# Keeping the low parts of weights in DRAM between the two halves of a two-layer decoder step

## The chip, the cores and the metric

The program runs on one core of one Trainium2 chip. The metric is the device time of one execution in microseconds (us), from start to end, with all weights read from DRAM. TensorE (PE) does the matrix products, VectorE (DVE), ScalarE (ACT) and GpSimd (POOL) the element work, and SyncE (SP) issues nearly all DMA transfers, one after the other in a fixed order.

## The reference, cut to what matters

Two layers are applied to 1024 prompt positions and 64 sample positions (1088 columns, T below). Layer 0 is an S5 state-space mixer and a gated delta network side by side; layer 1 is RWKV-7 time mixing. Each mixer is followed by a SwiGLU feed-forward network (FFN) of width 2816. Everything is in float32.

```python
def swiglu(h, w_gate, w_up, w_down):
    return (jax.nn.silu(h @ w_gate) * (h @ w_up)) @ w_down

for layer in range(2):
    h = rmsnorm(x, norm_mix[layer])
    mix = s5_and_gdn(h) if layer == 0 else rwkv7(h)   # each with input and output projections
    x = x + mix
    h = rmsnorm(x, norm_ffn[layer])
    x = x + swiglu(h, w_gate[layer], w_up[layer], w_down[layer])
y = rmsnorm(x, norm_final)
```

## The kernel before, in words

**Split products.** To reach float32 accuracy with TensorE's fp32r type, each operand is split: a high part that is the value rounded to fp32r, and a low part that is what the rounding left. A product is then three: high x high, high weight x low activation, low weight x high activation (`mm`, L301). So each weight tile that is loaded is split on chip. `weight` (L280) does this: SP loads the raw tile (L285) into one of two buffers `raw`, ACT rounds it into `wh` (L289), and POOL, or DVE where `lo=v` is given, subtracts to get `wl` (L290). `wh` and `wl` have three buffers for most weights; those of the down projection, named `wdh` and `wdl`, have two (L529).

**Two halves.** The 1088 columns are worked in two halves, `HALF` (L23): columns 0 to 511 as two chunks of 256, and 512 to 1087 as two chunks of 288. After the input stage of layer 0 (to about 456 us), the first loop of `trunk` (`for s in range(2)`) takes one half at a time through the output side of layer 0 (GLU, `wout`, FFN 0) and then the RWKV projections `wk`, `wr`, `wv` and the small low-rank weights `w1`, `a1`, `g1`. The second loop takes one half at a time through `wo` and FFN 1. Every weight is thus loaded and split twice, once for each half. By the weight loads of the trace the first half of loop one runs from 456 to 1359 us, the second from 1359 to 2435 us; loop two's halves run from 2435 to 3210 and from 3210 us to the end.

**FFN.** `ffn` (L455 on) works on 22 blocks of 128 hidden units. For each block there is a gate and an up weight, 128x1024 each (512 KB, matmuls `pg`); after each three blocks comes a down step with eight weights of 128x384 (192 KB, matmuls `pd`), in all seven such groups of eight and a last step with two large tiles. In FFN 0's first half DVE makes the `wdl` of these groups (`alone` is true, L529), in its second half POOL does.

**RWKV units.** While FFN 0's second half runs, the units of the RWKV scan of the first half are worked beside it (`unit`), and while FFN 1's first half runs, those of the second half. A unit loads its inputs (`rkb`, `th`, `ta`, `k`, `r`, `v`, about L1540 to L1549), inverts small triangular blocks with a chain of short DVE operations (L172 and L174, with round trips through DRAM: `dA`, `L`, `dT`, `Tc`), and then takes turns between PE and the other engines (L1652 to L1669).

**What sets the order.** The program is not written in the order in which it runs: a list scheduler simulates the engines and fixes the order of each engine's instructions when the program is built. On the chip each engine then takes its instructions strictly in that order, each waiting for the semaphores it names. A DMA on SP that waits therefore holds all that stand behind it.

Of the kernel before, what the change touches and what calls it, by code (L numbers as in the profile page):

```python
# [8 lines left out]
F32 = mybir.dt.float32  # L9
# [22 lines left out]
class Fine:  # L32


    def __init__(self, nc, pool, shape, ring=12, slots=None):
        self.nc, self.v, self.pool, self.shape, self.ring, self.n = nc, nc.vector, pool, list(shape), ring, 0
        self.slots = slots
# [38 lines left out]
    def log1p(self, out, e):  # L76

        v = self.v
        m, t, x = self.tmp(), self.tmp(), self.tmp()
        v.tensor_scalar(m, e, 0.41421356, None, op0=OP.is_gt)  # L80
        v.tensor_scalar(t, e, 0.5, 0.5, op0=OP.mult, op1=OP.add)
        v.tensor_mul(t, t, m)
        v.tensor_sub(x, e, t)
        p = self.horner(x, [7.0376836292e-2, -1.1514610310e-1, 1.1676998740e-1, -1.2420140846e-1, 1.4249322787e-1,
                            -1.6668057665e-1, 2.0000714765e-1, -2.4999993993e-1, 3.3333331174e-1, -0.5])
        v.tensor_mul(p, p, x)
        v.scalar_tensor_tensor(p, m, 0.69314718056, p, op0=OP.mult, op1=OP.add)
        v.tensor_add(out, p, x)


class Kern:
# [187 lines left out]

    def weight(self, src, kt=8, m=128, tag="w", bufs=3, lo=None):  # L280

        nc = self.nc
        raw = self.dp.tile([128, 1024], F32, tag="raw", name="raw", bufs=2)
        raw = raw[:, :kt * m].rearrange("p (k m) -> p k m", m=m)
        nc.sync.dma_start(raw, src)  # L285
        p = self.dx if tag == "wd" else self.dp
        wh = p.tile([128, kt, m], F32R, tag=tag + "h", name=tag + "h", bufs=bufs)
        wl = p.tile([128, kt, m], F32R, tag=tag + "l", name=tag + "l", bufs=bufs)
        nc.scalar.copy(wh, raw)  # L289
        (lo or nc.gpsimd).tensor_sub(wl, raw, wh)  # L290
        return wh, wl

    def mm(self, ps, w, x, cn, c=0):
# [1606 lines left out]
def loaded(K, s, dy, own=None):  # L1900

    t0, W, chunks = HALF[s]
    hs = [([], []) for c in chunks]
    for i, y in enumerate(dy):
        t = K.ring("act", "yr")[:, :W]
        e = own is not None and i == len(dy) - 1
        n = W - own.shape[-1] if e else W
        K.nc.sync.dma_start(t[:, :n], y[:, t0:t0 + n])
        for (c, cn), (h, l) in zip(chunks, hs):
            (a,), (b,) = K.hilo(1)  # L1910
            m = min(max(n - c, 0), cn)
            if m:
                K.split(a[:, :m], b[:, :m], t[:, c:c + m], K.nc.gpsimd if i % 2 else None)
            if m < cn:
                K.split(a[:, m:cn], b[:, m:cn], own[:, c + m - n:c + cn - n])
            h.append(a)
            l.append(b)
    return hs
# [5 lines left out]
@with_exitstack  # L1924
def trunk(ctx, tc, *aps):
    nc = tc.nc
    I = dict(zip(IN_NAMES, aps))
    I.update({"o_" + n: a for (n, _), a in zip(OUTS, aps[len(IN_NAMES):])})
    K = Kern(ctx, tc)
    K.nv = K.const.tile([128, 4, 8], F32, name="nv")  # L1930
    dr = ctx.enter_context(tc.tile_pool(name="tkd", bufs=1, space=DRAM))
    dx = dr.tile([128, 8, T], F32, name="dx")
    dyr = [dr.tile([128, T], F32, name="dyr%d" % i) for i in range(8)]
    right = ctx.enter_context(ExitStack())
    dyg, dy, second, early = layer0(K, I, right, dr)
    K.open(ctx, 288, 4, reuse_waits="tile")

    def tail(s, src, ys, w, i, x=None, done=None, ahead=lambda: None):
        if early is not None and s == i == 0:
            early.close()  # L1940
            K.open_more(ctx, reuse_waits="tile")
        x = K.load_x(src, s, x)
        first = s == i == 0
        ready = {}

        def gate():
            ready[0, 0] = K.weight(I["wg"][i][0])

        norms = K.project(x, ys, HALF[s][2], w, (lambda: None) if first else gate, 7 if first else 8)
        if first:  # L1950
            second(ORDER[0])
            with tc.high_priority(3000):
                norms = K.project_last(x, ys, HALF[s][2], w, gate)
            second(ORDER[1])
        return x, K.ffn(x, s, norms, K.nv[:, 1 + i], I["wg"][i], I["wup"][i], I["wd"][i], ready, ahead, s == i, done)

    rw = None
    for s in range(2):
        t0, W, chunks = HALF[s]
        wk0 = []  # L1960
        keys = lambda: wk0.append(K.weight(I["wk"][0]))
        keep = lambda m, c, cn, t: nc.sync.dma_start(dx[:, m, t0 + c:t0 + c + cn], t)
        x, norms = tail(s, I["x"], mixed0(K, s, dyg, dy, I["wglu"]), I["wout"], 0, done=keep, ahead=keys)
        if rw is None:
            right.close()
            rw = RWKV(K, ctx, I["rvec"])
            rw.open(ctx)
        unit = lambda ft, si=2 * s: rw.start(ft, si, I["rs0"], I["o_rwkv"], dyr)
        rw.projections(s, x, I["rsh"], *(I[n] for n in ("w1", "a1", "g1", "lw2", "wk", "wr", "wv")), unit, norms, wk0[0])
        for ft in range(8):  # L1970
            own = unit(ft, 2 * s + 1)
    nc.sync.dma_start(I["o_shift"], rw.shift)
    for s in range(2):
        t0, W, chunks = HALF[s]
        if s:
            K.psn = rw.norm_bank
        x, (bc, r1) = tail(s, dx, loaded(K, s, dyr, own if s else None), I["wo"], 1, rw.spare() if s else None)
        with tc.issue_after(K.last.ins) if s else ExitStack():
            for i, (c, cn) in enumerate(chunks):
                K.rms([t[:, c:c + cn] for t in x], K.nv[:, 3], K.spread(r1) if i else bc,  # L1980
                      lambda k, t: nc.sync.dma_start(I["o_y"][:, k, t0 + c:t0 + c + cn], t), True,
                      ((1, 3, 5, 7), (5, 7))[i] if s else ())
# [95 lines left out]
```

## Time and profile before

| | |
|---|---|
| median of 3 runs | 3781.07 us (3778.25 to 3793.54) |
| the profiled execution | 3776.02 us, of which the instructions span 3774.2 us |
| PE busy | 3475.1 us (92%) |
| DVE, ACT, POOL busy | 2512.1, 1390.7, 1317.6 us |
| mean granted PE clock | 0.941 of full speed |
| DMA | 356.35 MB, 94 GB/s on average |

The profile is one execution. Busy time of an engine counts its own instructions; matmuls are pipelined, so the duration of one (about 300 ns) is longer than the distance to the next (about 120 to 130 ns). A granted clock of 1.00 means 2.4 GHz and 0.50 means 1.2 GHz; a stretch's figure is the mean over it. In a timeline the bracket behind a row says how long the engine had been idle and what ended that.

### The profile page before, as it was taken

What the parts mean: (1) busy time and instruction counts of PE and PEld (TensorE: products, weight loads), DVE (VectorE), ACT (ScalarE), POOL (GpSimd) and SP (SyncE); (2) the same over time, 40 slices, a digit from 0 to 9 for tenths busy, and PEclk for the clock granted to TensorE, in tenths of its full rate; (3) what the DMA queues carried; (4) which work ended last, traced back from release to release, by engine and by line L of the source; (5) the groups of instructions that cost most, each with busy time, mean ns of one, the idle gap of its engine ahead of it and who ended that gap; (6) DMA issues with size and microseconds to landing.
All of it is one profiled execution on the core that took longest, in us unless ns stands there. A gap on an engine that the chain in (4) does not pass through costs nothing. (4 is left out here: it accounts for less than half of the span.)

```text
span 3774.2 us, 77080 instructions
## 1 busy us (share of the span) xinstructions
PE 3475.1 (92%) x29894; PEld 3221.5 (85%) x29894; DVE 2512.1 (67%) x6836; ACT 1390.7 (37%) x3264; POOL 1317.6 (35%) x1189
## 2 busy tenths in 40 slices
PE   7889989999988889999999988898998999899998
PEld 6879888899978788888888877888888888799997
DVE  7876877654456477777777674577787877553444
ACT  3333433322225443434433354443443443232222
POOL 3322233222236543433333264543333333332221
PEclk9989997999988999999999988998998999899999
DMA  4424442322223552222222224721222322322222
GB/s 104 94 81 132 97 124 75 95 81 90 88 92 96 167 174 68 60 79 79 78 81 69 92 72 129 222 84 50 86 86 78 94 82 87 130 62 82 90 77 70
DMA packets 331405, 356.35 MB, mean 94 GB/s; under 512 B 133272, under 2 KB 273304, under 8 KB 331040
## 3 DMA queue, kind: packets, MB, share of 16 engines
q1 hardware_dynamic: 321824, 342.52, 30.7%
q10 hardware_dynamic: 9216, 8.92, 0.7%
q8 instruction: 235, 3.85, 0.4%
q14 instruction: 130, 1.06, 0.1%
HBM read 285.34 MB, written 64.81 MB: 93 GB/s over the span
## 5 line engine op out<-in xcount | busy, mean ns | idle before, releaser
L290 POOL TENSOR_TENSOR wl<-raw,wh 128x1024 fp32r<-128x1024 f32 (+2 forms) x301 | 701.7, 2333 | 1094.9 <-ACT wh L289 1018.1
L301 PE MATMUL pg<-hi,wh 128*128 128x288 f32 (+1 forms) x2816 | 841.0, 299 | 31.5 <-DVE s L490 17.8
L301 PE MATMUL pg<-lo,wh 128*128 128x288 f32 (+1 forms) x2816 | 836.9, 297 | 4.8 <-DVE lo L388 3.5
L301 PE MATMUL pg<-hi,wl 128*128 128x288 f32 (+1 forms) x2816 | 835.6, 297 | 0.0
L301 PEld LDWEIGHTS pg<-hi,wh 128*128 128x128 f32 x2816 | 544.4, 193 | 43.9 <-DVE s L490 20.5
L301 PEld LDWEIGHTS pg<-lo,wh 128*128 128x128 f32 x2816 | 544.4, 193 | 14.2 <-DVE lo L388 4.7
L301 PEld LDWEIGHTS pg<-hi,wl 128*128 128x128 f32 x2816 | 544.1, 193 | 4.9 <-issue 2.1
L289 ACT CAST wh<-raw 128x1024 fp32r<-128x1024 f32 (+3 forms) x309 | 312.6, 1013 | 355.9 <-PE pg L301 88.4
L301 PE MATMUL pd<-ah,wdh 128*128 128x256 f32 (+1 forms) x1280 | 388.2, 303 | 18.6 <-DVE x L513 17.2
L301 PE MATMUL pd<-ah,wdl 128*128 128x256 f32 (+1 forms) x1280 | 373.2, 292 | 1.4 <-POOL wdl L290 1.4
L301 PE MATMUL pd<-al,wdh 128*128 128x256 f32 (+1 forms) x1280 | 371.9, 291 | 0.0
L301 PEld LDWEIGHTS pd<-ah,wdh 128*128 128x128 f32 x1280 | 243.9, 191 | 30.0 <-DVE x L513 19.6
L301 PE MATMUL pj<-lo,wh 128*128 128x256 f32 (+1 forms) x768 | 240.3, 314 | 18.8 <-DVE lo L388 15.9
L301 PE MATMUL pj<-hi,wh 128*128 128x256 f32 (+1 forms) x768 | 239.5, 314 | 14.0 <-ACT hi L387 6.0
L301 PEld LDWEIGHTS pd<-ah,wdl 128*128 128x128 f32 x1280 | 243.8, 190 | 3.4 <-POOL wdl L290 1.7
L301 PEld LDWEIGHTS pd<-al,wdh 128*128 128x128 f32 x1280 | 244.2, 191 | 1.1 <-issue 0.8
L301 PE MATMUL pj<-hi,wl 128*128 128x256 f32 (+1 forms) x768 | 234.9, 308 | 1.5 <-POOL wl L290 1.4
L513 DVE TENSOR_TENSOR x<-x,pd 128x256 f32<-128x256 f32 (+1 forms) x384 | 163.4, 427 | 87.7 <-PE pd L301 82.5
L289 ACT CAST wdh<-raw 128x384 fp32r<-128x384 f32 (+1 forms) x224 | 111.3, 497 | 247.0 <-PE pd L301 170.6
L172 DVE TENSOR_TENSOR Tm<-L,T 32x15 f32<-32x15 f32 (+8 forms) x600 | 181.7, 303 | 28.6 <-DMA L<-dA 15.3
L174 DVE TENSOR_TENSOR T<-T,Tm 32x15 f32<-32x15 f32 (+8 forms) x600 | 190.6, 318 | 13.5
L301 PE MATMUL pi<-hi,wh 128*128 128x272 f32 x640 | 192.2, 300 | 4.0 <-ACT us L1788 2.5
(643 smaller groups left out, 8275.5 us busy)
## 6 DMA issues: line engine op xcount, KB each, us to landing
raw<-in_wg SPq DMA_DIRECT2D x88, 512.0 KB
raw<-in_wup SPq DMA_DIRECT2D x88, 512.0 KB
raw<-in_wd SPq DMA_DIRECT2D x192, 192.0 KB
raw<-in_win SPq DMA_DIRECT2D x20, 512.0 KB
raw<-pr ACTq DMA_DIRECT2D x64, 136.0 KB
raw<-in_wk SPq DMA_DIRECT2D x16, 512.0 KB
raw<-in_wr SPq DMA_DIRECT2D x16, 512.0 KB
raw<-in_wv SPq DMA_DIRECT2D x16, 512.0 KB
```

What stands on the lines that cost most here:

```text
L172: v.tensor_mul(mm, L[:nl, j:j + 1, j + 1:16].to_broadcast([nl, j + 1, n]), T[:nl, 0:j + 1, j:j + 1].to_broadcast([nl, j + 1, n]))
L174: v.tensor_tensor(T[:nl, 0:j + 1, j + 1:16], T[:nl, 0:j + 1, j + 1:16], mm, op=op)
L289: nc.scalar.copy(wh, raw)
L290: (lo or nc.gpsimd).tensor_sub(wl, raw, wh)
L301: self.nc.tensor.matmul(ps, a[k], b[:, c:c + cn], start=i == 0, stop=i == last)
L513: v.tensor_add(x[m][:, c:c + cn], x[m][:, c:c + cn], ps)
```

## The change

A class `Kept` pairs a weight in DRAM with a second DRAM tensor of the same shape for its low part. The first time round, `weight` does what it did and then stores `wl` there with one more DMA on SP. Once the flag `there` is set, which the end of the first half of loop one does (for `wo`, its second use), `weight` loads `wl` from DRAM by SP in place of the subtraction; the raw tile is still loaded and ACT still rounds it. This concerns `wglu`, `wout`, `w1`, `a1`, `g1`, `wk`, `wr`, `wv`, `wo` and the three weights of FFN 0. FFN 1's weights are handled as before. In the built program 309 DMAs are added on SP, and 152 subtractions on POOL and 2 on DVE are gone.

```diff
+class Kept:
+    def __init__(self, src, low, root=None):
+        self.src, self.low, self.root = src, low, root or self
+        self.there = False
+    def __getitem__(self, i):
+        return Kept(self.src[i], self.low[i], self.root)
...
     def weight(self, src, kt=8, m=128, tag="w", bufs=3, lo=None):
         nc = self.nc
+        kept, src = (src, src.src) if isinstance(src, Kept) else (None, src)
         raw = self.dp.tile([128, 1024], F32, tag="raw", name="raw", bufs=2)
...
         nc.scalar.copy(wh, raw)
+        if kept and kept.root.there:
+            nc.sync.dma_start(wl.bitcast(F32), kept.low)
+            return wh, wl
         (lo or nc.gpsimd).tensor_sub(wl, raw, wh)
+        if kept:
+            nc.sync.dma_start(kept.low, wl.bitcast(F32))
         return wh, wl
...
+    both = ["wglu", "wout", "w1", "a1", "g1", "wk", "wr", "wv", "wo"]
+    for n in both:
+        I[n] = Kept(I[n], dr.tile(list(I[n].shape), F32, name="low_" + n))
+    for n in ("wg", "wup", "wd"):
+        I[n] = [Kept(I[n][0], dr.tile(list(I[n].shape[1:]), F32, name="low_" + n)), I[n][1]]
...
         for ft in range(8):
             own = unit(ft, 2 * s + 1)
+        for w in [I[n] for n in both[:-1]] + [I[n][0] for n in ("wg", "wup", "wd")]:
+            w.there = True
...
     for s in range(2):
         t0, W, chunks = HALF[s]
+        I["wo"].there = s > 0
```

The scheduler orders all engines anew. Three places follow. In the changed kernel the line numbers are higher: the raw load is L301, the load of a low part L307, the subtraction L309 and the store L311; the RWKV unit's lines are 21 higher.

The first is SP in a down group of FFN 0's first half, before and then changed; `wdl` is a low part of the down weight, `low_wd` its place in DRAM.

```order
L285 DMA raw<-in_wd 128x384 [waits DMAHW0_49,DVE_49]
L285 DMA raw<-in_wd 128x384 [waits DMAHW1_49,DVE_49]
L285 DMA raw<-in_wup 128x1024 [waits DMAHW2_49,DVE_49]
L285 DMA raw<-in_wg 128x1024 [waits DMAHW3_49,DVE_49]
L285 DMA raw<-in_wup 128x1024 [waits DMAHW4_49,Pool_49]
```

```order
L311 DMA low_wd<-wdl 128x384 [waits DMAHW2_49,DVE_49]
L301 DMA raw<-in_wd 128x384 [waits DMAHW7_49,Activation_49]
L311 DMA low_wd<-wdl 128x384 [waits DMAHW4_49,DVE_49]
L301 DMA raw<-in_wup 128x1024 [waits DMAHW1_49,Activation_49]
L311 DMA low_wd<-wdl 128x384 [waits DMAHW6_49,DVE_49]
L301 DMA raw<-in_wg 128x1024 [waits DMAHW3_49,Activation_49]
L311 DMA low_wup<-wl 128x1024 [waits DMAHW0_49,Pool_49]
```

A store now stands ahead of each raw load. It waits for the subtraction for which the raw load waited before.

The second is SP in a down group of FFN 0's second half, with the loads of an RWKV unit (`rkb` to `v`) among the weights, before and then changed.

```order
L285 DMA raw<-in_wd 128x384 [waits DMAHW5_49,Pool_49]
L178 DMA Tc<-dT 128x4x16 [waits DMAHW7_49,DMAHW1_49]
L1544 DMA rkb<-dks_13312 64x256 [waits DMAHW2_49,DVE_49,Pool_49]
L1544 DMA rkb<-dks_13312 64x256 [waits DMAHW3_49]
L1548 DMA th<-dth 128x256 [waits DVE_49]
L1549 DMA ta<-dta 128x256 [waits Activation_49]
L1540 DMA k<-dk 128x256 [waits DMAHW6_49,PE_49]
L1540 DMA r<-drr 128x256 [waits DVE_49]
L1540 DMA v<-dv 128x256 [waits DMAHW0_49,DVE_49]
L285 DMA raw<-in_wd 128x384 [waits DMAHW1_49,Pool_49]
```

```order
L307 DMA wdl<-low_wd 128x384 [waits DMAHW4_49,DMAHW0_49,PE_49]
L301 DMA raw<-in_wd 128x384 [waits DMAHW5_49,DMAHW1_49,Activation_49]
L1565 DMA rkb<-dks_13440 64x256 [waits DVE_49,Pool_49]
L1565 DMA rkb<-dks_13440 64x256
L1569 DMA th<-dth 128x256 [waits Activation_49]
L1570 DMA ta<-dta 128x256 [waits DVE_49]
L1561 DMA k<-dk 128x256 [waits DMAHW6_49,PE_49]
L1561 DMA r<-drr 128x256 [waits DMAHW7_49,DVE_49]
L1561 DMA v<-dv 128x256 [waits DMAHW0_49,DVE_49]
L307 DMA wdl<-low_wd 128x384 [waits DMAHW1_49]
L301 DMA raw<-in_wup 128x1024 [waits DMAHW2_49,Activation_49]
L307 DMA wdl<-low_wd 128x384 [waits DMAHW3_49,PE_49]
```

Before, only raw loads stand around the unit's loads; now a low part that PE has still to multiply by stands behind them, and each low part waits for PE to free its buffer.

The third is POOL beside the same units, before and then changed.

```order
L290 TENSOR_TENSOR wdl<-raw,wdh 128x384
L1588 TENSOR_TENSOR BK<-kp,Pi 64x4x64 x2
L290 TENSOR_TENSOR wdl<-raw,wdh 128x384
L1692 TENSOR_TENSOR yc<-yc,rs 128x256
L1573 TENSOR_TENSOR kp<-kp,k 128x256
L290 TENSOR_TENSOR wdl<-raw,wdh 128x384 x2
L290 TENSOR_TENSOR wl<-raw,wh 128x1024 x3
L1580 TENSOR_TENSOR AR<-rkb,P 64x4x64
L290 TENSOR_TENSOR wl<-raw,wh 128x1024
```

```order
L1609 TENSOR_TENSOR BK<-kp,Pi 64x4x64 x2
L1594 TENSOR_TENSOR kp<-kp,k 128x256
L1713 TENSOR_TENSOR yc<-yc,rs 128x256
L1601 TENSOR_TENSOR AR<-rkb,P 64x4x64
L1693 COPY Hs<-H 128x64
```

The unit's own POOL work stays; the subtractions among it are gone.

## Rows read from the trace of the kernel before

**Rows 1.** The page's first part: busy us, share of the span, instructions.

```profile
PE 3475.1 (92%) x29894; PEld 3221.5 (85%) x29894; DVE 2512.1 (67%) x6836; ACT 1390.7 (37%) x3264; POOL 1317.6 (35%) x1189
```

**Rows 2.** Busy time by stretch; the first line names the columns.

```profile
core 0: us, PE busy (x) PEld busy (x) DVE busy (x) ACT busy (x) POOL busy (x), PEclk, DMA share, GB/s
...
860.00:1090.00 230.00, 228.33 (x1914) 227.54 (x1912) 103.09 (x200) 63.29 (x116) 57.29 (x24) 1.00 0.30 90
...
1200.00:1359.00 159.00, 138.06 (x980) 128.01 (x979) 78.45 (x138) 74.38 (x168) 84.73 (x87) 0.92 0.58 186
1359.00:1571.00 212.00, 193.72 (x1756) 174.86 (x1755) 166.14 (x487) 92.22 (x238) 83.13 (x69) 0.94 0.25 74
1571.00:2098.00 527.00, 502.69 (x4601) 461.21 (x4601) 392.92 (x1182) 208.15 (x559) 178.58 (x178) 0.99 0.26 76
2144.00:2435.00 291.00, 251.43 (x1713) 231.82 (x1714) 174.14 (x368) 133.56 (x293) 161.07 (x173) 0.88 0.46 144
```

**Rows 3.** Waits of PE, 1359 to 2435 us: us in total, times, longest.

```profile
PE pc L1652 <- DVE XV L1663: 11.6, 11, 1.9
PE pd L301 <- DVE x L513: 7.7, 7, 1.7
```

**Rows 4.** Groups on POOL, 1359 to 2435 us: busy, mean ns, idle before.

```profile
L290 POOL TENSOR_TENSOR wl<-raw,wh 128x1024 fp32r<-128x1024 f32 x78 | 188.8, 2421 | 215.7 <-ACT wh L289 199.3 <-DMA dx<-x 12.7 <-PE pj L301 1.5
L290 POOL TENSOR_TENSOR wdl<-raw,wdh 128x384 fp32r<-128x384 f32 x48 | 49.6, 1034 | 60.8 <-ACT wdh L289 57.0 <-POOL AR L1580 2.0 <-PE pc L1652 1.1
```

**Rows 5.** Timeline around one PE gap in FFN 0's second half: start, us, what.

```profile
1928.87 2.40 POOL L290 TENSOR_TENSOR wl<-raw,wh 128x1024 fp32r<-128x1024 f32 x1 [0.82 <-PE pT L1695]
1928.90 2.40 DVE L172 TENSOR_TENSOR Tm<-L,T 32x15 f32<-32x15 f32 x1 [0.53 <-DMA L<-dA]
...
1931.18 0.29 PE L301 MATMUL pg<-hi,wl 128*128 128x288 f32 x1
...
1932.92 0.49 PE L1652 MATMUL pc<-XV,AR 128*128 128x128 f32 x2 [1.44 <-DVE XV L1663]
```

**Rows 6.** Line L172, 1571 to 2098 us: least, median and longest ns.

```profile
L172 DVE TENSOR_TENSOR Tm<-L,T x165: 160/199/2452, 1608.2 to 2082.1; 32x15 f32<-32x15 f32 x22, 32x28 f32<-32x28 f32 x22, 32x39 f32<-32x39 f32 x22, 32x48 f32<-32x48 f32 x22
```

**Rows 7.** Timeline of SP, ACT, DVE in a down group, FFN 0's first half.

```profile
924.00 0.56 DVE L290 TENSOR_TENSOR wdl<-raw,wdh 128x384 fp32r<-128x384 f32 x1
924.59 6.68 SPq L285 DMA_DIRECT2D raw<-in_wd  x4
925.58 0.51 ACT L289 CAST wdh<-raw 128x384 fp32r<-128x384 f32 x1 [1.62 <-PE pd L301]
927.67 0.51 ACT L289 CAST wdh<-raw 128x384 fp32r<-128x384 f32 x1 [1.57 <-PE pd L301]
...
933.06 0.33 SPq L285 DMA_DIRECT2D raw<-in_wup  x1
...
936.63 1.05 ACT L289 CAST wh<-raw 128x1024 fp32r<-128x1024 f32 x1 [2.06 <-DMA raw<-in_wup]
```

**Rows 8.** Timeline: issue of a raw down weight, and the cast that waited.

```profile
961.90 3.93 SPq L285 DMA_DIRECT2D raw<-in_wd  x3
...
964.28 0.52 ACT L289 CAST wdh<-raw 128x384 fp32r<-128x384 f32 x1 [1.71 <-DMA raw<-in_wd]
```

**Rows 9.** Waits of DVE, 1090 to 1359 us: us, times, longest.

```profile
DVE bv L1596 <- DMA v<-dv: 13.5, 1, 13.5
```

**Rows 10.** Timeline of ACT in FFN 1's second half: two down weights.

```profile
3380.55 0.51 ACT L289 CAST wdh<-raw 128x384 fp32r<-128x384 f32 x1 [1.87 <-PE pd L301]
3382.89 0.51 ACT L289 CAST wdh<-raw 128x384 fp32r<-128x384 f32 x1 [1.83 <-PE pd L301]
```

**Rows 11.** Timeline of SP: one unit's loads, first and last.

```profile
1819.39 0.32 SPq L1548 DMA_DIRECT2D th<-dth  x1
...
1820.28 1.09 SPq L1544 DMA_DIRECT2D rkb<-dks  x2
...
1825.44 0.32 SPq L1540 DMA_DIRECT2D v<-dv  x1
```

**Rows 12.** Waits of SP's queue, 1571 to 2098 us: us, times, longest.

```profile
SPq L285 <- POOL wdl L290: 94.1, 35, 12.2
...
SPq L1544 <- DVE AR L1580: 60.9, 7, 11.5
```

More of the change, by code (lines that the diff above doesn't have):

```diff
@@ L88, in log1p, with rearrange @@
         v.tensor_add(out, p, x)
+class Kept:
[4 more added lines that the diff above has]
+        return Kept(self.src[i], self.low[i], self.root)
+    def rearrange(self, p):
+        return Kept(self.src.rearrange(p), self.low.rearrange(p), self.root)
 class Kern:
```

## Prediction, made before the changed kernel was run

> **What bounds the kernel now.** I read the page's busy shares first: PE is at work for 92% of the span, so time can come only from PE's gaps and from stretches at the lower clock; POOL's share is about a third [rows 1]. The view by stretch comes next, since the change touches stretches with different limits [rows 2]. FFN 0's first half in its steady part (860 to 1090) leaves PE 230.0 - 228.33 = 1.7 us idle: nothing can be won there, and whatever comes late shows at once. In the second half of loop one PE idles 212 - 193.72 = 18.3 us (GLU, `wout`, start of FFN 0), 527 - 502.69 = 24.3 us (FFN 0) and 291 - 251.43 = 39.6 us (RWKV projections), 82.2 us in all. The waits of PE tell for whom: its largest ones in that half end with DVE, not with POOL [rows 3].
>
> DVE's lateness has a cause that the timeline shows. In the example a subtraction `wl` on POOL runs from 1928.87 for 2.40 us, and a small DVE operation that starts beside it also takes 2.40 us; PE runs out of matmuls 2.6 us later and idles 1.44 us until the next RWKV step has its `XV` from DVE [rows 5]. The same line of DVE has a median of 199 ns and a longest of 2452 ns [rows 6]. So a DVE operation that meets a POOL subtraction can last as long as it, and the RWKV chain behind it is late by up to 2.4 us.
>
> **The second half loses the subtractions.** POOL's 78 large ones (188.8 us) and 48 of the down weights (49.6 us) go [rows 4], some 238 us with the two main shapes. POOL itself is not waited for, so this time is worth nothing directly. What it frees is DVE: the stretched operations. Their price is bounded from below by nothing, since the same order could leave PE another late partner, and from above by the 82.2 us of gaps. In the FFN and GLU stretches (18.3 + 24.3 = 42.6 us), where the example is typical, I take 60%: 25.5 us. In the projections (39.6 us) PE also waits for DVE's and ACT's own splitting of activations, which the change leaves; a quarter, 10 us. Sum 35.5 us.
>
> The granted clock adds to it. At 0.94, 0.99 and 0.88 the three stretches lose 0.06 x 212 + 0.01 x 527 + 0.12 x 291 = 52.9 us of full-speed PE time [rows 2]. Fewer gaps should hold the clock up more; I take a quarter, 13 us (bounds 0 and 52.9). Gain of the second half: 48.5 us.
>
> **The second half gains loads of low parts.** A low part of a down weight has two buffers, so its load can be issued only when PE is done with the weight two before, and must land while PE works on the one between. That one takes PE 2.34 us, the distance of two casts released by PE where nothing lies between [rows 10]. A 192 KB load takes 964.28 - 961.90 = 2.38 us from issue to its cast [rows 8]. Alone these balance, and RWKV steps between the weights give slack; before, cast and subtraction took 0.51 + 1.03 us [rows 4, 10]. So in quiet places I charge nothing. But in six of the seven groups the seven loads of an RWKV unit stand on SP between two low parts, as the second order shows. Their issues took 6.4 us, 1819.39 to 1825.76, waits included [rows 11]. Six of them take about 0.4 us each and `rkb` 1.09 us for two, so some 3.1 us without waits. A low part behind them is issued 0.33 + 0.4 + 3.1 = 3.8 us after its predecessor and lands at 6.2 us. PE, which needs it after two weights with an RWKV step in each, some 2 x 3 = 6 us (estimated from the 2.34 us with 0.6 us of RWKV work), waits 0.2 us, plus what the unit's loads wait. These waited up to 11.5 us each, seven times in this stretch, 60.9 us in all [rows 12]; but they waited for DVE, which now is late less often, so I take 2 us. That makes 6 x 2.2 = 13 us. Bounds: 0, and with the old waits 6 x (0.2 + 8.7) = 53 us.
>
> For the three-buffered weights two large weights lie between, and I charge nothing; that cover would be gone only if a unit's loads held SP for over 10 us. ACT's casts and the raw loads stay, and raw loads come earlier, because their buffer no longer waits for POOL.
>
> **The first half gains stores.** On SP a store waits for the subtraction for which the raw load behind it waited anyway, so no new wait arises; new are its issue (0.33 us) and its bytes ahead of the next raw load. Two down weights now go round in cast 0.51, subtraction 0.56, issue, landing 2.38 and 0.1 us of hand-overs: 3.6 us against PE's 2 x 2.1 = 4.2 us [rows 7, 8]. 192 KB cost about 0.7 us: the 512 KB load took 936.63 - 933.06 = 3.57 us, 1.19 us more for 320 KB [rows 7, 8]. With the store the round is 3.6 + 0.33 + 0.7 = 4.6 us, 0.4 us over PE's pace; over three rounds 1.2 us. The `wup` load behind the group then comes up to 2.2 us late, in a stage with no slack. I take 1.3 us for each of seven groups, 9 us (bounds 0 and 7 x 2.2 = 15 us). In the projections DMA is already busy 0.58 of the time at 186 GB/s [rows 2], and DVE once waited 13.5 us for a unit's `v` [rows 9]; sixteen stores of 512 KB there, and the small stores of the low-rank weights, I charge 3 us, bounds 0 and 20. First half: 12 us.
>
> The Trainium skill, page "Perfetto Trace Analysis", section DMA Optimizations, advises giving inputs and outputs separate issuing engines, which this change does not do. By that rule the 0.33 us of issue would leave each round, 4.3 in place of 4.6 us, and most of the 9 us would go; no row here shows these weights with stores on another queue, so the trace cannot say.
>
> **Sum.** -48.5 + 13 + 12 = -23.5 us. The profiled execution took 3776.0 us, so 3752.5; the median of the runs shown lies 5.05 us above it, so about 3758 us, 0.6% under the median. What can be told from no change is 0.5%, 19 us: the limits are 3762 and 3800 us.
>
> **Rivals.**
>
> *The gain is spent again.* The order of every engine is new, and PE takes its order strictly; a DVE that is free sooner helps only where PE's next RWKV step stands for it. For it: the RWKV chain keeps its round trips through DRAM and its long DVE sequence, and the new waits on SP lie in the same chain. Against it: the gap of the example is directly the length of a subtraction. With half of the 48.5 us won and the 25 us of costs kept, the time is 3776 - 24 + 25 + 5 = 3782 us, no change.
>
> *SP holds the low parts back; slower.* The place is a down group of FFN 0's second half with a unit's loads in it; the price is the 53 us above, if those loads wait as long as they did, plus the lower clock after stalls of several us, which I put at 3 us for each of six groups, 18 us. It decides from a wait of about 6 us per unit on. Then 3776 - 48.5 + 12 + 53 + 18 + 5 = 3816 us. For it are the long waits of rows 12; against it, that they ended with a DVE which was itself slowed by POOL.
>
> *Loads land later under load; slower too.* The loads add some 28 MB (36 of 512 KB and 48 of 192 KB) to the 527 us of FFN 0's second half, which lifts its 76 GB/s to about 130 [rows 2]. If a landing grows by 1 us with that, each of 56 down weights is late by 2.38 + 1 - 2.94 = 0.44 us: 25 us more, 3783 us, and with 2 us more, 81 us, 3839 us. Against it: 130 GB/s is below the 186 GB/s at which another stretch runs [rows 2]. The Trainium skill, page "DMA: Bandwidth & Descriptors", section Latency and other measured facts, gives an access to DRAM as 0.2 us on average and 2 us at high load, which would be the second figure; no row here shows a landing that grew so far.
>
> *All of it is won.* PE keeps 10 of the 82.2 us of gaps, half of the clock's 52.9 us comes back and the costs stay at 10 us: 3776 - 72 - 26 + 10 + 5 = 3693 us.
>
> **How the numbers follow.** Forecast (a gain of 5 to 50 us) 0.46; spent again 0.22; held back on SP 0.16; late landing 0.08; all won 0.08. Part of the forecast's case lies within 0.5%, and so does most of the second: faster 0.45, same 0.28, slower 0.27. The likeliest case's own range is 3730 to 3775 us. The range over the cases leaves out half of "all won" below and about half of the two slow cases above: 3705 to 3815 us.
>
> **What would show it.** Right: POOL's busy time falls by some 240 us, the longest L172 in FFN 0's second half falls to well under 2.4 us, PE's gaps between the second half's start and `wo` fall from 82 to about 50 us with new waits for `wdl`, and 860 to 1090 grows by a few us with ACT waiting for raw loads behind stores. Wrong: PE gaps of over 3 us before `pd` matmuls that end with a `wdl` load, with SP waiting for DVE ahead of it; or gaps as long as before although L172 is short, which would make the order and not POOL their cause; or a first half that grows by over 20 us.

## The result, and the profile after

The changed kernel takes 3727.99 us (median of 4 runs, 3716.72 to 3733.62) against 3780.47 us of the kernel before on the same chip. The ratio is 0.9853 with a 95% interval of 0.983 to 0.9875: faster by 1.5%, some 52 us, where 22.5 us were forecast. That is 2 us under the likeliest case's own range (3730 to 3775 us) and inside the range over the cases (3705 to 3815 us). The profiled execution took 3726.54 us.

The page's first part after [rows 1]: POOL lost 276 us of work, DVE 135 us, though the change took only two operations from DVE.

```profile
PE 3456.1 (93%) x29894; PEld 3211.8 (86%) x29894; DVE 2377.6 (64%) x6834; ACT 1393.8 (37%) x3264; POOL 1041.9 (28%) x1037
```

Busy time by stretch after, with the columns of rows 2: FFN 0's first half in its steady part, the start of the second half (GLU, `wout`, start of FFN 0), its FFN 0, and its projections. Each stretch holds the same number of matmuls as that of rows 2, within ten.

```profile
859.00:1095.00 236.00, 229.89 (x1914) 227.99 (x1914) 103.63 (x200) 63.75 (x117) 57.17 (x24) 1.00 0.54 176
...
1375.00:1570.00 195.00, 187.73 (x1754) 171.79 (x1753) 140.13 (x479) 93.57 (x237) 39.02 (x49) 0.95 0.46 144
1570.00:2075.00 505.00, 500.74 (x4609) 462.31 (x4607) 323.85 (x1186) 210.42 (x555) 49.80 (x95) 1.00 0.45 135
...
2110.00:2397.00 287.00, 246.00 (x1706) 227.30 (x1707) 146.79 (x364) 133.00 (x293) 89.89 (x139) 0.90 0.59 191
```

In FFN 0's second half PE idles 505 - 500.74 = 4.3 us where it idled 24.3 us [rows 2], and before it 195 - 187.73 = 7.3 us in place of 18.3. DVE is busy 69 us less in FFN 0 with as many operations (1186 for 1182). In the projections PE idles 41.0 us, as before (39.6). FFN 0's first half takes 236 us in place of 230. The line that was 199 ns in the median and 2452 ns at the longest [rows 6] is now, in FFN 0's second half:

```profile
L186 DVE TENSOR_TENSOR Tm<-L,T x164: 155/196/215, 1565.1 to 2058.7; 32x63 f32<-32x63 f32 x22, 32x55 f32<-32x55 f32 x22, 32x48 f32<-32x48 f32 x22, 32x39 f32<-32x39 f32 x22
```

The waits of PE in that stretch (us in total, times, longest) hold one wait for a low part, of 0.2 us. The largest one that is left, for DVE, is 1.2 us, and the wait for `XV` at the head of rows 3 is not among them:

```profile
PE pd L322 <- DVE x L534: 1.2, 2, 0.8
...
PE pd L322 <- DMA wdl<-low_wd: 0.2, 1, 0.2
```

On SP the waits of the unit's `rkb` loads for DVE fell from 60.9 us in seven [rows 12] to 22.8 us in eight:

```profile
SPq L1565 <- DVE AR L1601: 22.8, 8, 10.1
```

In the second half's projections PE's gaps are as long as before, and waits for loaded low parts are among them (`low_wr`, `low_wk`), which the kernel before did not have:

```profile
PE pj L1388 <- ACT kks L1404: 9.0, 6, 3.2
PE pj L322 <- DMA wl<-low_wr: 6.9, 5, 1.8
...
PE pj L322 <- DMA wl<-low_wk: 3.4, 3, 2.1
```

### The profile page after: what moved, and what is told of

Same layout as the page of the kernel before. It is cut to its first block, busy times and chain, and to the rows that moved or that the text cites. A ratio compares the mean times of both kernels' runs of the same rounds, so it can differ in the third digit from the quotient of the medians.

```text
span 3724.8 us, 77416 instructions
## 1 busy us (share of the span) xinstructions
PE 3456.1 (93%) x29894; PEld 3211.8 (86%) x29894; DVE 2377.6 (64%) x6834; ACT 1393.8 (37%) x3264; POOL 1041.9 (28%) x1037
## 5 line engine op out<-in xcount | busy, mean ns | idle before, releaser
L309 POOL TENSOR_TENSOR wl<-raw,wh 128x1024 fp32r<-128x1024 f32 (+3 forms) x205 | 480.4, 2347 | 924.0 <-ACT wh L305 864.6
L322 PEld LDWEIGHTS pg<-lo,wh 128*128 128x128 f32 x2816 | 540.7, 192 | 13.5 <-DVE lo L409 6.3
L322 PE MATMUL pi<-lo,wh 128*128 128x272 f32 x640 | 190.4, 297 | 0.0
L322 PE MATMUL pi<-hi,wl 128*128 128x272 f32 x640 | 190.1, 297 | 0.0
```

Source lines behind the costliest of these rows:

```text
L322: self.nc.tensor.matmul(ps, a[k], b[:, c:c + cn], start=i == 0, stop=i == last)
```

## The experiments

All kernels issue the same number of matmuls, 29894, so stretches can be cut after the same count of matmuls in every trace. (The order of the matmuls differs a little from kernel to kernel, so a cut does not always fall on the very same one.) The table gives lengths in us, under the names of the places where the cuts lie in the kernel before. The median is that of each kernel's runs; a ratio below compares with runs of the kernel before, whose medians lie between 3780.5 and 3783.6 us.

| kernel | median | 456-860 | 860-1304 FFN 0, proj., half 1 | 1304-1571 to FFN 0, half 2 | 1571-2144 FFN 0, half 2 | 2144-2435 proj., half 2 | 2498-3160 FFN 1, half 1 | 3210-3286 `wo`, half 2 |
|---|---|---|---|---|---|---|---|---|
| before | 3780.5 | 401.8 | 444.1 | 267.0 | 573.2 | 290.7 | 662.1 | 76.0 |
| changed | 3728.0 | 402.0 | 457.6 | 253.4 | 545.8 | 288.8 | 651.3 | 66.5 |
| stores alone | 3810.5 | 401.8 | 455.8 | 280.5 | 572.5 | 290.2 | 669.1 | 76.2 |
| loads alone | 3704.4 | 399.7 | 446.7 | 249.4 | 545.0 | 286.0 | 645.6 | 67.6 |
| idle subtraction | 3809.5 | 401.3 | 455.2 | 275.0 | 582.2 | 310.7 | 650.1 | 69.0 |
| writes only | 3742.1 | 400.7 | 455.5 | 256.1 | 547.2 | 294.0 | 650.4 | 71.2 |
| no projections | 3739.5 | 401.0 | 451.6 | 249.6 | 545.5 | 293.8 | 674.2 | 68.6 |
| stores later | 3728.5 | 399.9 | 454.3 | 251.1 | 545.9 | 287.4 | 658.3 | 62.8 |
| later with pieces | 3727.1 | 407.7 | 446.0 | 254.1 | 541.7 | 291.4 | 642.8 | 67.5 |
| half stores | 3801.9 | 417.8 | 450.6 | 277.3 | 574.6 | 292.5 | 653.8 | 70.4 |
| split stores | 3793.3 | 409.1 | 463.3 | 278.0 | 573.8 | 293.3 | 643.4 | 75.8 |
| double stores | 3789.8 | 390.9 | 471.1 | 273.0 | 568.7 | 289.5 | 654.3 | 72.0 |
| loads twice | 3819.7 | 401.5 | 453.8 | 261.6 | 605.8 | 327.2 | 657.2 | 68.3 |
| pieces 256 (all) | 3720.4 | 402.6 | 439.4 | 261.3 | 553.4 | 289.8 | 626.7 | 77.1 |
| pieces 256 (from GLU) | 3704.2 | 395.1 | 437.8 | 266.7 | 554.3 | 288.7 | 617.6 | 69.7 |
| changed + pieces 256 | 3679.0 | 399.1 | 447.5 | 248.6 | 541.8 | 291.5 | 631.3 | 69.7 |
| pieces 128 (from GLU) | 3679.9 | 395.2 | 442.8 | 257.7 | 551.7 | 286.9 | 613.5 | 69.7 |
| changed + pieces 128 | 3668.7 | 383.0 | 454.7 | 253.4 | 546.2 | 291.7 | 618.2 | 72.1 |

### Cost and gain apart

*Stores alone.*

```diff
-        if kept and kept.root.there: ...   # the load of the low part
-        if kept:
+        if kept and not kept.root.there:
             nc.sync.dma_start(kept.low, wl.bitcast(F32))
```

> The stores alone: the first half stores the low parts, the second half subtracts on POOL as before and loads nothing more. Theory A (the stores cost what the two traces show between 860 and 1304 us, +6 in FFN 0 and +8 in the projections, and the second half has all its old waits): 3780 + 14 = 3794 us, 3786 to 3800. Rival B (the 14 us belong to the place of the work and are given back where the first half ends, as the 15 us won between 1304 and 1456 suggest): 3780 us, within 5. Theory A also says that the stretch from the second half's FFN 0 on is the kernel before's, gaps of 24 us in the 527 us included.

3810.51 us, ratio 1.0071 (1.0056 to 1.0086): 27 us more, above both theories. 860 to 1304 grew by 11.7 us, near the 14 of theory A; 1304 to 1571, where the eight `wv` stores lie, grew by 13.5.

*Loads alone.*

```diff
-            nc.sync.dma_start(wl.bitcast(F32), kept.low)
+            nc.sync.dma_start(wl.bitcast(F32), self.one[:, :kt * m]...)
...
-        if kept:
-            nc.sync.dma_start(kept.low, wl.bitcast(F32))
+        if kept and kt * m == 1024 and not self.put:
+            nc.sync.dma_start(self.one, ...)
```

> The loads alone: the first half stores one low part only, and the second half loads this one in place of each weight's own low part, so what the second half computes with the weights is changed; DMAs of the second half are as many and as large as in the changed kernel. Theory A: 3728 - 14 = 3714 us, 3705 to 3720. Rival B (stores cost nothing in the end): 3728 us. Rival C (all loads come from the same 512 KB of DRAM, and this makes them slower): over 3735 us.

3704.42 us, ratio 0.9793 (0.9778 to 0.9809): 79 us less, a little under theory A's range. -79 + 27 = -52 us, the whole change: cost and gain add up, and by these two runs both are more than twice what was forecast (35.5 net for the second half, 12 for the stores). Other amounts of stores, below, cost 9 to 21 us, so 27 is the price in this kernel and not a fixed one.

### What POOL's subtraction does to DVE

*Idle subtraction.*

```diff
             nc.sync.dma_start(wl.bitcast(F32), kept.low)
+            (lo or nc.gpsimd).tensor_sub(raw, raw, wh)
             return wh, wl
```

> As the changed kernel, but in the second half the engine that subtracted before does so still, into the raw weight's own buffer, where nobody reads the result; the matmuls take the loaded low part. Theory A (the gain is that POOL's subtractions no longer lengthen DVE operations that run beside them): the gain of FFN 0 (32 us) and of the stretches at its sides and at wo (15 and 12 us) is gone and the stores stay, 3780 to 3794 us, taken 3788; the longest L186 operation is near 2.4 us again, and the gaps of PE in FFN 0's second half near 24 us. Rival D (the gain is that the low part is there sooner, and that POOL's queue is no longer ahead of it): 3728 us, within 6, since no matmul waits for POOL.

3809.49 us, ratio 1.0061 (1.0038 to 1.0084). Theory A's mechanism holds and D falls: subtractions whose results nobody reads cost 81 us, all of the gain and more. The time is 15 us over A's range; the projections, at 310.7 us, are 20 us longer than with loads or subtractions alone (288.8 and 290.7), and why is open. The stretch of FFN 0's second half and the DVE line in it:

```profile
1589.00:2125.00 536.00, 512.84 (x4604) 467.06 (x4603) 397.02 (x1181) 210.40 (x556) 182.79 (x179) 0.98 0.43 127
```

```profile
L186 DVE TENSOR_TENSOR Tm<-L,T x165: 154/197/2453, 1626.5 to 2110.7; 32x15 f32<-32x15 f32 x22, 32x28 f32<-32x28 f32 x22, 32x39 f32<-32x39 f32 x22, 32x48 f32<-32x48 f32 x22
```

DVE is back at 397 us, the longest operation at 2453 ns, PE's gaps at 536 - 512.84 = 23.2 us. Only `wo` keeps its shorter time (69 us), so at least part of its gain has another cause.

*Writes only.*

```diff
             nc.sync.dma_start(wl.bitcast(F32), kept.low)
+            for n in (kt, kt, kt // 2):
+                (lo or nc.gpsimd).memset(raw[:, :n], 0.0)
             return wh, wl
```

> As the run with the idle subtraction (3809 us), but where that subtracted, the engine only writes zeros into the raw weight's buffer, two and a half passes of it, so that it is busy about as long and gives the buffer back as late, and reads no SBUF. Theory A (what lengthens DVE operations is that POOL reads two operands from SBUF): 3728 us, 3718 to 3740, DVE busy 324 us in FFN 0's second half as in the changed kernel, no L188 operation near 2.4 us. Rival F (the loss of 81 us came from POOL's time: its own later work, or the raw buffers given back by POOL and not by ACT): 3800 to 3815 us, with DVE busy well under 397 us there.

3742.12 us, ratio 0.9884 (0.9864 to 0.9904), 2 us over theory A's range and far from F's; the interval overlaps the changed kernel's. The stretch and the line:

```profile
1565.00:2065.00 500.00, 494.88 (x4608) 456.42 (x4607) 330.05 (x1184) 211.12 (x561) 183.30 (x344) 1.00 0.46 136
```

```profile
L186 DVE TENSOR_TENSOR Tm<-L,T x165: 154/196/621, 1600.8 to 2046.6; 32x15 f32<-32x15 f32 x22, 32x28 f32<-32x28 f32 x22, 32x39 f32<-32x39 f32 x22, 32x48 f32<-32x48 f32 x22
```

POOL is as busy as with the subtraction (183.30 against 182.79 us) and gives the raw buffers back after as much work, yet DVE needs 330 us in place of 397, near the 324 of the changed kernel, where POOL does neither. So neither POOL's time nor the raw buffers, but what POOL does with SBUF costs DVE: subtracting does, writing hardly. The writes are also shorter instructions, and short subtractions help too, as the next runs show. But the longer writes take 0.95 us each:

```profile
L309 POOL MEMSET raw<- 128x1024 f32 x70 | 66.7, 953 | 100.6 <-ACT wh L305 95.5 <-issue 2.7
```

Subtractions of 0.49 us, half of that, leave DVE at 355 us (pieces of 128x128 below), so shortness alone does not explain 330. This is the rule of the Trainium skill, page "SBUF — State Buffer", section Who interferes with whom: a DVE instruction with two SBUF inputs contends with a GpSimd instruction that reads SBUF, not with one that only writes it. The two rows agree (397 and 330 us); what DVE itself reads was not varied in any run.

*Pieces.* On the kernel before:

```diff
-        (lo or nc.gpsimd).tensor_sub(wl, raw, wh)
+        for k in range(0, kt, kt if lo else 2):
+            q = slice(k, min(k + (kt if lo else 2), kt))
+            (lo or nc.gpsimd).tensor_sub(wl[:, q], raw[:, q], wh[:, q])
```

> As the kernel before, but each of POOL's subtractions is cut into pieces of 128x256 (four of about 0.73 us for one of 2.39). Theory A1 (a DVE operation with two SBUF operands stands still until POOL's running instruction ends): the longest L174 operation falls from 2.45 to about 0.9 us, DVE busy in FFN 0's second half falls from 393 us to between 330 and 375, and the time to 3755 us, 3740 to 3772. Rival A2 (both engines only share a rate as long as both are at work): longest still near 2.4 us, DVE busy 390 us or more, POOL's operations longer, 3780 to 3800 us.

3720.35 us, ratio 0.9831 (0.9812 to 0.9851): as fast as the change, with no DRAM at all. FFN 0's second half, the DVE line, and the pieces on POOL (busy, mean ns):

```profile
1578.00:2085.00 507.00, 493.97 (x4595) 454.75 (x4593) 367.65 (x1181) 208.54 (x560) 208.15 (x331) 1.00 0.28 79
```

```profile
L174 DVE TENSOR_TENSOR T<-T,Tm x165: 156/203/752, 1613.8 to 2069.4; 32x15 f32<-32x15 f32 x22, 32x28 f32<-32x28 f32 x22, 32x39 f32<-32x39 f32 x22, 32x48 f32<-32x48 f32 x22
```

```profile
L292 POOL TENSOR_TENSOR wl<-raw,wh 128x256 fp32r<-128x256 f32 x140 | 102.7, 764 | 88.8 <-ACT wh L289 81.1 <-PE pg L303 5.2 <-ACT s L491 2.5
```

The longest DVE operation is now as long as a piece (752 against 764 ns): it stands still until POOL's running instruction ends. Theory A1 holds, A2 falls. (The Trainium skill, page "SBUF — State Buffer", section SBUF: two separate sides, has it so: the one that starts first holds the shared ports for its whole instruction, and the other is blocked. The 752 ns agree.) POOL is busier than before (208 us, 179 in rows 2) and DVE still 25 us less. The time is 20 us under A1's range: I forgot FFN 1, which is also subtracted, and 2498 to 3160 fell by 35 us. Against it, the first 458 us, with the mixer's input weights, took 17 us more.

### The stores

*Stores later*, and *later with pieces* of 128x256 in all that POOL still subtracts.

```diff
         nc.sync.dma_start(raw, src)
+        self.stored()      # issues the store of the weight before
...
-            nc.sync.dma_start(kept.low, wl.bitcast(F32))
+            self.late.append((kept.low, wl.bitcast(F32)))
```

> As the changed kernel, but a low part's store is issued one weight later, behind the next weight's raw load, so that SP no longer stands at a wait for POOL's subtraction between two raw loads. Theory G (the stores cost 27 us because SP waits for POOL before each and issues the next raw load late): 3701 to 3715 us, with the FFN 0 stretch from 860 us back at 230 us. Rival H (they cost it as traffic: bytes, DMA engines that the loads share): 3722 to 3734 us, that stretch still 235 us.

> Both edits in one: the changed kernel with stores issued one weight later and POOL's subtractions of the first half cut into pieces of 128x256. Under theories A1 and G: 3690 to 3705 us. Under A1 and H: 3715 us, under A2 and G: 3705 to 3720 us, under A2 and H: 3728 us or more.

3728.51 us, ratio 0.985 (0.9833 to 0.9866), and 3727.09 us, 0.9848 (0.9833 to 0.9862). The first looks like theory H, but the edit did not do what it was meant to. In the changed kernel the scheduler had already put nearly every store behind the next weight's raw load (store, raw load, store, raw load, as in the order before the rows), and the edit leaves that order almost as it was. SP stands as long for the subtractions. Its waits (us, times, longest) from 860 to about 1310 us in the kernel before, then in the changed kernel and in the one with later stores:

```profile
SPq L285 <- POOL wl L290: 105.1, 32, 7.9
SPq L285 <- DVE wdl L290: 67.6, 30, 7.2
```
```profile
SPq L311 <- POOL wl L309: 98.4, 31, 7.7
SPq L311 <- DVE wdl L309: 62.0, 30, 11.0
```
```profile
SPq L319 <- POOL wl L310: 95.4, 30, 7.7
SPq L319 <- DVE wdl L310: 60.5, 31, 11.0
```

So this run decides nothing between G and H. The first pair of lines speaks against G: without any stores SP stood 172.7 us for the same subtractions, at its raw loads, and with them 160.4. The second kernel fits neither G with A1 nor H with A1: its 19 us more in the first 458 us hide what the pieces gain (FFN 1's stretch 643 us).

*Half, split, double stores*, each on the kernel with the stores alone.

```diff
+            nc.sync.dma_start(kept.low[:, :kt // 2], wl[:, :kt // 2].bitcast(F32))
```
```diff
+            for q in (slice(0, kt // 2), slice(kt // 2, kt)):
+                nc.sync.dma_start(kept.low[:, q], wl[:, q].bitcast(F32))
```
```diff
             nc.sync.dma_start(kept.low, wl.bitcast(F32))
+            nc.sync.dma_start(kept.two, wl.bitcast(F32))
```

> As the run with the stores alone (3810 us), but each store writes half of its low part: as many DMAs, half the bytes. Nothing reads them, and the second half subtracts as before. If the 27 us are bytes that share the DMA engines with the raw loads: 3797 us, 3790 to 3803. If they are issue time and waits of SP, by count: 3806 to 3814 us.

> As the run with the stores alone, with each store issued as two of half its size: the bytes the same, the DMAs twice as many. By bytes: 3810 us, 3803 to 3816. By count and issue time: 3825 to 3838 us.

> As the run with the stores alone (3810 us), with each low part stored a second time, to another place in DRAM; twice the stores and twice the bytes. If the cost of 27 us goes by the amount stored: 3838 us, 3826 to 3850. If it is a cost of having a store at all between the loads (SP's wait for the subtraction, paid once): 3810 to 3820 us.

3801.88 (1.0032 to 1.0072), 3793.33 (1.0021 to 1.005) and 3789.82 us (1.0009 to 1.0036). The half stores lie where the theory of bytes had them; the split and the double stores lie under both of their theories, and twice the stores took less time than one. So the totals answer to no theory. The stretch with most of the stores, 860 to 1304 in the kernel before, tells more: half, whole, split and double stores in this order, one row from each trace, columns as in rows 2.

```profile
875.00:1325.50 450.50, 408.77 (x3197) 391.44 (x3196) 229.09 (x447) 163.44 (x344) 174.25 (x159) 0.92 0.44 135
```
```profile
860.40:1316.20 455.80, 410.23 (x3198) 393.21 (x3197) 226.46 (x447) 162.84 (x344) 175.30 (x159) 0.92 0.53 171
```
```profile
862.30:1325.60 463.30, 414.73 (x3197) 396.30 (x3196) 229.97 (x447) 163.36 (x344) 174.45 (x159) 0.91 0.54 168
```
```profile
851.00:1322.10 471.10, 416.09 (x3198) 396.81 (x3196) 219.64 (x472) 163.92 (x346) 176.80 (x163) 0.91 0.69 232
```

Against 444.1 us without stores that is +6.5, +11.7, +19.2 and +27.0 us. Here the cost grows with the bytes (half to whole) and with the number of DMAs (whole to split). What the totals lose or win beside it lies elsewhere. 1304 to 1571, with the `wv` stores, is 10.3, 13.5, 11.0 and 6.0 us longer, in no order of dose; 456 to 860, where the stores begin, varies between 390.9 and 417.8 us in these four kernels, and FFN 1's first half between 643.4 and 674.2 us among kernels that treat FFN 1's weights alike. What sets these swings of some 15 us to either side off stays open.

*No projections.*

```diff
-    both = ["wglu", "wout", "w1", "a1", "g1", "wk", "wr", "wv", "wo"]
+    both = ["wglu", "wout", "wo"]
```

> As the changed kernel, with only the GLU's, the mixer output's (wout, wo) and FFN 0's low parts kept; the seven projection weights are subtracted in both halves, and stored in neither. Theory A (stores between 1090 and 1304 cost 8 us, the second half's projections won nothing): 3720 us, 3714 to 3726, with 30 us less of low granted clock in the first half's projections. Rival E (the projections' loads did win, hidden by the transfers' waits of 10 us that came in their place): 3728 to 3738 us, with PE's gaps between the start of the second half's projections and wo over 45 us.

3739.5 us, ratio 0.9887 (0.9872 to 0.9902), above both ranges, by 1.5 us for E. Against the changed kernel, 860 to 1304 is 6 us shorter and the projections' second half 5 us longer: keeping these weights about pays for itself, no more. PE's gaps of over 45 us (E) did not come, they are 42. What makes the total 11.5 us longer is FFN 1's first half, 674 us for 651, so the total settles nothing.

### Low parts behind other transfers on SP

*Loads twice.*

```diff
+            for i in range(2):
                 nc.sync.dma_start(wl.bitcast(F32), kept.low)
```

> As the changed kernel, with each low part loaded twice into the same buffer: SP holds every later transfer back once more, by the landing of the first load. Forecast's own mechanism (SP holds low parts back and PE waits for them): new PE waits for wl and wdl of over 20 us in FFN 0's second half, 3750 to 3790 us. Theory S (the low parts land so early that as much again stays hidden): 3726 to 3740 us, PE's gaps in FFN 0's second half under 8 us.

3819.73 us, ratio 1.0116 (1.0091 to 1.0141), 92 us above the changed kernel and 30 us over the range of the forecast's own mechanism: theory S falls. PE's waits in FFN 0's second half, and SP's own:

```profile
PE pd L323 <- DMA wdl<-low_wd: 20.7, 23, 1.7
```

```profile
SPq L308 <- DMA wdl<-low_wd: 77.6, 44, 3.2
SPq L308 <- DMA wl<-low_wup: 36.7, 17, 3.4
SPq L308 <- DMA wl<-low_wg: 35.3, 13, 4.2
```

SP stands 150 us at the second loads, 1.8 us each for `wdl` (77.6 / 44), and PE waits 20.7 us for `wdl` in 23 places in place of 0.2. The mechanism of the forecast exists, but the change itself stays within the cover, that is, the time PE needs anyway until it comes to the low part.

### A version that beats both

*Pieces of 128x256 from the GLU on*, the same with the change, *pieces of 128x128*, and these with the change.

```diff
-        (lo or nc.gpsimd).tensor_sub(wl, raw, wh)
+        n = 2 if bufs == 3 or tag == "wd" and not lo else kt      # 1 for pieces of 128x128
+        for k in range(0, kt, n):
+            q = slice(k, min(k + n, kt))
+            (lo or nc.gpsimd).tensor_sub(wl[:, q], raw[:, q], wh[:, q])
```

> The kernel before with POOL's subtractions cut into pieces of 128x256, but only for the weights from the GLU on (GLU, mixer output, both FFNs, projections, wo); the first mixer's input weights are subtracted whole, since the run with all in pieces lost 17 us of its 63 back in the first 458 us. Theory A1: 3703 us, 3695 to 3712. Rival I (the 17 us are no cost of the pieces but of where the instructions fell, and come back elsewhere): 3720 us.

> The changed kernel with the same pieces, from the GLU on. The change leaves POOL's subtractions in the first half and in FFN 1, so pieces are left to win there: theory A1 gives 3728 - 12 (FFN 1) - 10 (the first half's end and projections) = 3706 us, 3698 to 3718, no better than the pieces alone. Rival J (the two gains add: 55 + 80): below 3680 us.

> The kernel before with pieces of 128x128 from the GLU on (eight of about 0.52 us for one of 2.39). Theory A1: longest L175 operation about 0.55 us, yet POOL's time per weight grows from 2.39 to 4.1 us, and a DVE operation meets a piece as often as POOL is busy: 3697 to 3712 us, the same as with pieces of 128x256. Rival K (the low parts now come too late): over 3720 us, with PE waits for POOL's wl over 15 us.

> The changed kernel with the subtractions that POOL still does cut into pieces of 128x128, from the GLU on (with pieces of 128x256 it took 3679 us; pieces of 128x128 without the change 3680). Theory A1 (what is left of the change beside fine pieces is that DVE meets no piece at all in the second half; against it stand the stores): 3660 us, 3648 to 3675. Rival M (with fine pieces the change has nothing left to win and its stores cost 27): 3680 to 3707 us.

3704.2 us (0.9766 to 0.9815); 3679.04 us (0.9708 to 0.9751); 3679.91 us (0.9714 to 0.9755); 3668.69 us (0.9683 to 0.9729). The first is as expected. The second came out under A1's range, just at J's limit: the gains add more than I thought. The third beat its range, and K falls. Its DVE line, stretch and pieces on POOL:

```profile
L172 DVE TENSOR_TENSOR Tm<-L,T x169: 155/203/621, 1551.2 to 2052.6; 32x48 f32<-32x48 f32 x23, 32x39 f32<-32x39 f32 x23, 32x28 f32<-32x28 f32 x23, 32x15 f32<-32x15 f32 x23
```

```profile
1551.00:2060.00 509.00, 501.58 (x4601) 462.99 (x4600) 355.46 (x1189) 211.09 (x554) 243.55 (x524) 1.00 0.27 79
```

```profile
L293 POOL TENSOR_TENSOR wl<-raw,wh 128x128 fp32r<-128x128 f32 x281 | 128.2, 491 | 79.6 <-ACT wh L289 76.3 <-PE pg L304 2.7
```

DVE is at 355 us in place of 369 with larger pieces, though POOL is busy 244 us. The fourth is the fastest, 2.9% under the kernel before, inside A1's range and under M's 3680. Still, its interval overlaps those of the second and third, and of the 11 us between it and the third 12 lie in 456 to 860 (383.0 for 395.2), where the change only adds stores. So that the change adds anything to fine pieces is not shown.

## Why the prediction was right in sign and wrong in size

The forecast of the trace was -23.5 us, measured were -49.5. By stretch, with the terms put where they belong (the clock's 13 us as 4.5 before and 8.7 in the projections, which rounds to -23.7 in all):

| stretch | forecast | measured |
|---|---|---|
| 860-1304, stores | +12 | +13.5 |
| 1304-2144: DVE's share -25.5, clock -4.5, low parts held back +13 | -17 | -41.0 |
| 2144-2435: projections -10, clock -8.7 | -18.7 | -1.9 |
| all else | 0 | -20.1 |

In the second half of loop one (1304 to 2435) the sum came out near, -42.9 for -35.7 us, but because its errors cancel: up to the end of FFN 0 it won 24 us too little, in the projections 17 us too much. It is luck too that PE's gaps fell from 82 to 7.3 + 4.3 + 41.0 = 53 us, near the 50 named as a sign. Of the 26 us beyond the forecast 20 lie in stretches for which the sum had no term.

- **What bounds it, and the mechanism**: right. That DVE stands still beside POOL's subtraction, and PE behind it, is shown by the idle subtraction, the writes and the pieces together.
- **The step that failed: low parts that SP holds back, +13 us.** PE waited 0.2 us for them. The sum had a low part behind a unit's loads issued 3.8 us after its predecessor, 2 us later with the unit's own waits, and PE needing it 6 us after that predecessor's issue. One such place after the change, first on SP, then PE's last matmul with the weight two before, the first with the weight between, and the first with the low part in question:

```profile
1766.54 0.32 SPq L307 DMA_DIRECT2D wdl<-low_wd  x1
...
1772.99 0.42 SPq L307 DMA_DIRECT2D wdl<-low_wd  x1
```
```profile
1769.79 0.29 PE L322 MATMUL pd<-ah,wdl 128*128 128x288 f32 x1
...
1772.00 0.30 PE L322 MATMUL pd<-ah,wdl 128*128 128x288 f32 x1
...
1779.08 0.30 PE L322 MATMUL pd<-ah,wdl 128*128 128x288 f32 x1
```

SP's part of the sum was about right: 6.5 us from issue to issue for 5.8 forecast, and 22.8 us of `rkb` waits in eight units, 2.9 each for 2. PE's was wrong: it came to the low part 12.5 us after the predecessor's issue (1779.08 - 1766.54), not after 6, for it had that much other work between: it idled 4.3 us in the whole stretch. With the 2.38 us of a landing, 3.7 us were to spare. In the four places of this kind in that stretch the issue came 6.0 to 7.8 us after the predecessor's and PE's first use 10.6 to 12.5 us after it. (The sum's "six of them take about 0.4 us" should be five; its 3.1 us are right.)

- **60% of 42.6 us**: too little. Of the 18.3 and 24.3 us of gaps 11.0 and 20.0 went, 73%. PE's busy time fell beside it, for about the same matmuls, from 193.72 to 187.73 and from 502.69 to 500.74 us, some 8 us for the 4.5 of the clock. I had read the share from one example; the idle subtraction would have told it.
- **Projections, -18.7 us**: wrong. PE's gaps stayed (39.6 us before, 41.0 after), the granted clock rose only from 0.88 to 0.90, and 10.3 us of waits for `low_wr` and `low_wk` are new: here, at 191 GB/s, some low parts do come late, for which the sum charged nothing ("for the three-buffered weights ... I charge nothing"). Subtracting these weights again made this stretch only 5 us longer (no projections, 293.8 for 288.8).
- **Stores, +12 us**: the total is right for their stretch by 1.5 us, its parts are not: 6 us in FFN 0 for 9 forecast, and about 8 in the projections for 3. As a whole the stores cost 27 us in the run with the stores alone; 13.5 of them lie in 1304 to 1571, with the eight `wv` stores that the sum left out, and this part does not follow the dose. That no new wait arises on SP is borne out: it stood 172.7 us for the subtractions before and 160.4 after. What issuing the stores on another engine would give wasn't tried.
- **All else, -20.1 us**: put at nothing, for `wo` without a reason, since the change loads its low parts too. FFN 1's first half (-10.8), whose weights the change does not touch, is within its spread among these kernels, so that share of the gain is luck. For `wo` (-9.5) the cause is open: it stays short with the idle subtraction, and 70 us occur without loaded low parts too.
- **Rivals**: "spent again" is out by its price. "Held back on SP" names a real mechanism, which showed only at twice the loads. "Loads land later" did not come in FFN 0 (0.2 us of waits for low parts at 135 GB/s), but the projections have some of it. "All won" (3693 us) was nearest for the loads by themselves (3704 us), though the projections kept their gaps.

## What to carry to other kernels

When a slow engine's share looks free because nobody waits for it, look at the longest against the median of the small operations on the other engines: 2452 against 199 ns said that POOL's work was paid on DVE. Before moving such work to DRAM, cut it: four or eight short instructions in place of one long won at least as much as the change without a byte of traffic, not least because they also help where the weights are used for the first time. Two kernels of this kind, each scheduled anew, can differ by 15 us to either side in stretches that the edit doesn't touch; judge a cost in the stretch where it acts, and by its dose. And look in the built order whether an edit has moved anything: the later stores had not.

## What the hardware did unexpectedly

POOL's subtractions cost the kernel time although PE hardly ever waits for POOL: 152 of them more or less, nearly all in the second half of loop one, moved the kernel by 81 us, through DVE operations of 0.2 us that lasted up to 2.45 us. Cutting each into pieces of 128x128 makes POOL work longer (179 to 244 us in FFN 0's second half) and the kernel shorter by 101 us. And a second load of 192 KB into the same buffer, which waits for the first to land, stopped SP for 1.8 us on average.
